# A hybrid attention, convolution and mixture-of-experts layer: the work ahead of the experts in another order, the output gate behind the projection, and softmax and convolution on other engines

## The chip, the cores and the metric

The kernel runs on one core of a Trainium2 chip. The metric is the device time of one execution in microseconds (us). The core's engines are named as in the profile: PE (TensorE: matrix products and transposes), DVE (VectorE), ACT (ScalarE), POOL (GpSimd) and SP (SyncE, which issues nearly all of the transfers). Each engine works through its own list of instructions in the order in which they were written; semaphores hold an instruction back until what it reads is there. The whole list is written by hand here: the code's order is the order on each engine.

## What is computed

One layer on 256 latent tokens (x) and 256 context tokens, 1024 features wide, all float32. It has two parts: a mixer with three groups of heads, and 32 experts.

```python
def trunk_layer(x, xc, mod_x, mod_c, norm1, norm2, w_in, w_fourier, w_conv, rpb, w_out,
                w_rg, b_rg, w_re, b_re, w_gate, w_up, w_down, last):
    ...
    sh1, sc1, g1, sh2, sc2, g2 = jnp.split(mod_x[:, None, :], 6, axis=-1)
    ...
    ux = (rms_norm(x, norm1) * (1 + sc1) + sh1) @ w_in
    uc = (rms_norm(xc, norm1) * (1 + csc1) + csh1) @ w_in
    fx, qx, kx, vx, bx, cx, hx = split_in(ux)
    fc, qc, kc, vc, bc, cc, hc = split_in(uc)
    attn_x = na_latent(qx * scale, kx, vx, kc, vc, rpb)
    conv_x = bx * short_conv(cx * hx, w_conv)
    x = x + g1 * mix_out(fx, attn_x, conv_x, w_fourier, w_out)
    ...
    hx2 = rms_norm(x, norm2) * (1 + sc2) + sh2
    if last:
        y = hier_moe(hx2.reshape(-1, d), w_rg, b_rg, w_re, b_re, w_gate, w_up, w_down)
        x = x + g2 * y.reshape(b, n, d)
```

Here `mod_x = silu(c) @ w_ada + b_ada`, 6144 columns; `w_in` is 1024 x 2560 (256 Fourier, 3 x 512 attention in 8 heads of 64, 3 x 256 convolution); `na_latent` is a softmax over a band of neighbours with a learned bias and all context keys; `short_conv` has width 3; `fourier_mix` is the real part of a two-dimensional Fourier transform, followed by a 256 x 256 product; `w_out` is 1024 x 1024. Each token goes to 2 of the 32 experts (gate and up 1024 x 512, down 512 x 1024 each). The weights of the experts are some 200 MB, all are read once, and the last step is an RMS norm.

## The kernel before

**Weights** come through ten slabs of 2 MB in SBUF (16 KB in each partition). `pump` starts loads in the order of a list, `queue`, as long as a slab is free: `ada0` and `in_0`, `in_1` (first modulation, Fourier columns, outer gate of the convolution, keys), `in_3` (values), `ada1` (four slabs: the gate g1 and the shift of the second norm), `in_2` (queries), `in_4` (the convolution's operands), `small` (constants of the Fourier part and space for intermediate results), `ada2` (four slabs: scale of the second norm and g2), `out_0`, `out_1`, and then for each expert `gu0`, `gu1`, `dn`. `drop` gives a slab back when its last reader is written. A list element that finds no slab holds all that follow, since SP issues in order. An eleventh slab, `more`, is opened shortly before the experts.

**Products with split operands.** Weights of `w_in` and `w_out` are cut into a high and a low part: ACT casts a chunk of 128 x 1024 to a rounded format (L343), DVE subtracts (L344), and the pair lies in one of three buffers `ws`. `ahead(n)` writes casts and splits up to the n-th chunk. `project(i, c, ...)` multiplies a chunk of the input projection by the modulated tokens in three terms (L360), `mix(n)` a chunk of the output projection by the mixer's result `cat` (L517); `mixed` writes two parts of a row block of `cat` (cast on ACT L409, difference on DVE L410).

**Sums.** The modulation that is not needed first is made on DVE: `sums(n)` adds n weighted rows of a slab into an accumulator of 128 x 1024 (L317; L315 for a first row), `acc` for `ada1` and `acc2` for `ada2`; `sum_rows` adds the partitions on PE (L329), `columns` turns a row into columns, and `spread` puts a row on all partitions.

**Attention.** Four pairs of heads. `scores` makes on PE four tiles of 128 x 512 (L467); DVE adds the bias and takes the maximum (two instructions a tile, L473 and L475), ACT the exponential and its sum (L476), DVE the reciprocal (L480) and multiplies by it, the shares (L481). `ptrans` transposes the shares on PE (L488) and ACT copies them to SBUF (L489), `pv` multiplies by the values (L496).

**The order around the change.** Values, queries and the convolution's operands are projected with DVE sums between; then `scores(0, 1)`, the convolution on POOL (L548 to L552), the Fourier products (L539, L544, L569), and the other pairs with the output projection between. POOL multiplies `w_out` by the gate g1 in place (`fold`, L504) before it is cast, so that the projection's result is gated. `x1(t)` adds the residual for half of the tokens (L640), transposes, and makes the second norm (L646, L198, L199); `logits`, `route` and `place` choose the experts; `group` gathers tokens with products (L761), and `hidden` (L792) and `project_down` (L814) are the experts.

## Time and profile before

| what | value |
|---|---|
| median of 3 runs | 645.34 us (644.65 to 646.25) |
| span of the profiled execution | 641.5 us |
| median less span: what lies around the span | 3.84 us |
| PE busy | 476.4 us, 74% |
| DVE busy | 226.8 us, 35% |
| ACT busy | 144.8 us, 23% |
| POOL busy | 44.5 us, 7% |
| moved by DMA | 246.12 MB, mean 384 GB/s |

The span runs from the first to the last instruction of one profiled execution, and shares are of that span. They are averages over two unlike parts: the work ahead of the experts, up to about 204 us, and the experts, which are two thirds of the span. The chain that ended last is, by the page, 62% DMA, 26% PE and 8% DVE.

### The profile page before, as it was taken

How to read it: one execution, taken by the hardware profiler on the slowest of the kernel's cores; microseconds unless marked ns; L12 is line 12 of the kernel's file. 1: busy time of each engine (PE TensorE's matmuls, PEld its weight loads, DVE VectorE, ACT ScalarE, POOL GpSimd, SP SyncE). 2: the span in 40 equal slices, each digit the busy share in tenths (PEclk: the TensorE clock that was granted, in tenths of full speed). 3: DMA queues.
4: the chain of work that ended last, by engine and by line, in shares of the span. 5: the costliest groups of instructions: out<-in, count | busy, mean ns of one | idle time of the engine just before them, and what ended most of it. 6: DMA issues, size and time to landing. Idle time of an engine off the chain costs nothing.

```text
span 641.5 us, 11030 instructions
## 1 busy us (share of the span) xinstructions
PE 476.4 (74%) x4775; PEld 307.9 (48%) x4775; DVE 226.8 (35%) x525; ACT 144.8 (23%) x322; POOL 44.5 (7%) x44
## 2 busy tenths in 40 slices
PE   3999999887987887585567555855946585568785
PEld 3787898544775454253235222632523253235442
DVE  4767877999744222021011000211210021012323
ACT  4524234454642111011001000110100011003003
POOL 1000000894000000000000000000000000000000
PEclk9999999888997999898779778797888888789798
DMA  9999579953797999999999999999999999999992
GB/s 351 422 419 360 222 277 372 428 230 147 295 399 297 429 426 424 426 426 427 426 427 423 425 430 423 422 425 426 424 428 426 425 429 424 426 426 428 423 381 102
DMA packets 21220, 246.12 MB, mean 384 GB/s; under 512 B 2214, under 2 KB 3242, under 8 KB 6956
## 3 DMA queue, kind: packets, MB, share of 16 engines
q1 hardware_dynamic: 21016, 245.08, 91.9%
q8 instruction: 39, 0.64, 0.4%
q10 hardware_dynamic: 148, 0.27, 0.1%
q14 instruction: 17, 0.14, 0.1%
HBM read 244.28 MB, written 1.05 MB: 382 GB/s over the span
## 4 chain that ended last, share of the span: by engine, by line
DMA 62%; PE 26%; DVE 8%; ACT 1%; issue 1%; SPq 1%; DVEq 0%; ACTq 0%
DMA gu<-in_w_gu 41%; DMA dn<-in_w_dn 18%; PE b L360 11%; PE m L792 3%; DMA ada<-in_w_ada 3%; PE b L517 2%; DVE f L317 2%; DVE acc L481 2%; PE m L761 1%; PE m L814 1%; DVE ws L344 1%; PE b L261 1%; PE b L488 1%; PE m L951 1%; DVE acc L475 1%
## 5 line engine op out<-in xcount | busy, mean ns | idle before, releaser
L792 PE MATMUL m<-gu,xg 128*32 128x256 f32 x2048 | 139.9, 425 | 63.8 <-DMA gu<-in_w_gu 60.2
L792 PEld LDWEIGHTS m<-gu,xg 128*32 128x32 f32 x2048 | 72.9, 120 | 125.5 <-DMA gu<-in_w_gu 43.3
L814 PE MATMUL m<-dn,ht 128*32 128x256 f32 x992 | 74.3, 450 | 26.7 <-DMA dn<-in_w_dn 19.6
L802 DVE TENSOR_TENSOR hh<-m,sg 128x128 f32<-128x128 f32 x32 | 9.3, 291 | 182.0 <-ACT sg L800 182.0
L814 PEld LDWEIGHTS m<-dn,ht 128*32 128x32 f32 x992 | 38.8, 125 | 50.5 <-issue 38.5
L822 DVE COPY yg<-m 32x256 f32<-32x256 f32 x56 | 23.4, 418 | 99.1 <-PE m L814 86.8
L822 ACT COPY yg<-m 32x256 f32<-32x256 f32 x56 | 20.4, 364 | 142.8 <-DVE yg L822 142.8
L360 PE MATMUL b<-uh,ws 128*128 128x256 f32 (+1 forms) x224 | 52.1, 317 | 0.1
L800 ACT ACTIVATE sg<-m 128x128 f32<-128x128 f32 x32 | 8.9, 278 | 161.2 <-PE m L792 161.2
L360 PEld LDWEIGHTS b<-uh,ws 128*128 128x128 f32 x224 | 37.0, 188 | 4.7 <-issue 1.2
L360 PE MATMUL b<-ul,ws 128*128 128x256 f32 (+1 forms) x112 | 35.1, 313 | 0.0
L769 POOL TENSOR_TENSOR sw<-st,cmb 128x256 f32<-128x256 f32 x8 | 5.8, 725 | 418.4 <-DVE st L694 293.4
L783 PE MATMUL m<-yg,sl 128*128 128x512 f32 x56 | 27.7, 639 | 6.4 <-ACT yg L822 6.4
L761 PEld LDWEIGHTS m<-sr,xs 128*128 128x128 f32 x224 | 28.7, 208 | 7.7 <-PEq L887 4.8
L761 PE MATMUL m<-sr,xs 128*128 128x128 f32 x224 | 28.9, 292 | 4.0 <-DVE sr L754 4.0
L344 DVE TENSOR_TENSOR ws<-in,ws 128x1024 fp32r<-128x1024 f32 x20 | 24.4, 1221 | 14.9 <-ACT ws L343 14.8
L767 DVE TENSOR_SCALAR xg<-m,a,sh 128x128 f32<-128x128 f32 x32 | 13.1, 410 | 45.4 <-PE m L761 36.9
L804 PE MATMUL m<-ident,hh 128*128 128x128 f32 x32 | 10.9, 340 | 23.7 <-DVE hh L802 23.7
L765 ACT ACTIVATE xg<-m,sh,a 128x128 f32<-128x128 f32 x32 | 14.6, 458 | 59.4 <-DVE xg L767 59.4
L360 PE MATMUL b<-ws,uh 128*128 128x512 f32 (+1 forms) x96 | 25.9, 354 | 1.9 <-ACT uh L300 1.9
L517 PE MATMUL b<-ws,cat 128*128 128x512 f32 x96 | 24.3, 402 | 0.0
L804 PEld LDWEIGHTS m<-ident,hh 128*128 128x128 f32 x32 | 4.6, 143 | 40.9 <-DVE hh L802 40.8
(236 smaller groups left out, 574.4 us busy)
## 6 DMA issues: line engine op xcount, KB each, us to landing
gu<-in_w_gu SPq DMA_DIRECT2D x63, 2048.0 KB, 39.2
dn<-in_w_dn SPq DMA_DIRECT2D x31, 2048.0 KB, 39.1
ada<-in_w_ada SPq DMA_DIRECT2D x12, 2048.0 KB, 9.0
in<-in_w_in SPq DMA_DIRECT2D x3, 2048.0 KB, 11.3
in<-in_w_in SPq DMA_DIRECT2D x8, 512.0 KB, 17.2
out<-in_w_out SPq DMA_DIRECT2D x2, 2048.0 KB, 10.8
gu<-in_w_gu SPq DMA_DIRECT2D x4, 512.0 KB, 32.5
dn<-in_w_dn SPq DMA_DIRECT2D x3, 512.0 KB, 11.5
```

The source lines that it names most:

```text
L317: DVE.scalar_tensor_tensor(a, w, scx[:, j:j + 1], a, op0=OP.mult, op1=OP.add)
L344: DVE.tensor_tensor(ws[:, 1], src, ws[:, 0].bitcast(F32), OP.subtract)
L360: PE.matmul(po, wv if wst else uv, uv if wst else wv, start=(j == 0 and m == 0 and n == 0), stop=(j == NJ - 1 and m == len(parts) - 1 and ...
L517: PE.matmul(yo[t, h], cat[:, a, MIX[n], blk(t)], ws[:, b, h, :], start=(first and k == 0), stop=(last and k == 2))
L761: PE.matmul(pg[:, j, :], xs[:, t, jj * P:(jj + 1) * P], sr[:, t], start=(t == 0), stop=(t == 1))
L765: ACT.activation(xg[:, jj, :], pg[:, j, :], AF.Identity, bias=sh2[:, 0, jj:jj + 1], scale=a2[:, 0, jj:jj + 1])
L767: DVE.tensor_scalar(xg[:, jj, :], pg[:, j, :], a2[:, 0, jj:jj + 1], sh2[:, 0, jj:jj + 1], op0=OP.mult, op1=OP.add)
L783: PE.matmul(yp[2 * t + h], sl[:, t, :], yg[:, blk(h, 512)], start=(g == 0), stop=(g == NE // 4 - 2))
L792: PE.matmul(pg[32 * q:32 * q + 32], xg[:, j, CAP * i:CAP * (i + 1)], wgu[j // 4][:, :, j % 4, q * P:(q + 1) * P], start=(j == 0), stop=(j ...
L804: PE.transpose(pt, hh, ident)
L814: PE.matmul(pd[32 * q:32 * q + 32, :], ht[:, 32 * k:32 * k + 32], wdn[:, q, k, :], start=(k == 0), stop=(k == 3))
L822: (ACT.copy if q % 2 else DVE.tensor_copy)(dst, src)
```

## The change

- **Gate behind the projection.** `fold` is gone; g1 is spread on all partitions late (after pair 3's scores are written) and `x1` multiplies the projection's result by it before the residual is added: one more DVE operation for each half row. The rows of g1 and of the shift are summed in two steps of 256 columns.
- **Shares on ACT.** `shares(m)` holds the reciprocals on DVE and the multiplication as an ACT activation with a scale per partition (L512 of the changed kernel). Half of the PSUM copies of `ptrans` go from ACT to DVE, as does one of the two query copies.
- **Convolution on DVE**, with multiply-and-add in one instruction (`convolve`, L549 to L556).
- **Fourier group beside the values:** `channels`, `positions` and `fourier` stand between the chunks of the value projection, and the `small` operands are loaded earlier for it.
- **Pairs interleaved:** `scores(0)` stands after the first of the four convolution chunks, `scores(1)` before the last, and shares, transposes, sums, casts and products of the pairs follow in turn. All twelve rows of `ada2` that are summed on DVE are summed after the first scores; before, eight of them stood ahead of the attention.
- Not tied to these: the additions of the bias band are half as many and twice as wide, and `sums` stand elsewhere between the values and queries.

```diff
-    queue += [("in", 3, w_in[3])] + first[0:2] + [("in", 2, w_in[2]), first[2], ("in", 4, w_in[4]), first[3]]
-    queue += [("small", 0, small_b)] + [("ada2", t, w_ada[8 + t]) for t in range(2)]
+    queue += [("in", 3, w_in[3]), ("small", 0, small_b)] + first[0:2] + [("in", 2, w_in[2]), first[2], ("in", 4, w_in[4]), first[3]]
+    queue += [("g2", 0, b_g2)] + [("ada2", t, w_ada[8 + t]) for t in range(2)]
...
-    for c in range(4):
-        project(3, c, vals)
-        sums(3)
+    project(3, 0, vals)
+    sums(2)
+    project(3, 1, vals)
+    sums(2)
+    channels()
+    positions()
+    project(3, 2, vals)
+    sums(3)
+    fourier()
+    project(3, 3, vals)
+    sums(3)
...
         project(2, c, quer)
-        sums(1)
+        sums(2 if c < 2 else 1)
...
+    def shares(m):
         for t in range(2):
-            for h in hs:
-                p, mx = pb2[h % 2][:, t, :], ms[h, t]
+            for hh in range(2):
+                p, mx = pb2[hh][:, t, :], stats(2 * m + hh, t)
                 DVE.reciprocal(mx[:, 3:4], mx[:, 2:3])
-                DVE.tensor_scalar(p, p, mx[:, 3:4], None, op0=OP.mult)
...
+                ACT.activation(p, p, AF.Copy, scale=mx[:, 3:4])
...
-                ACT.copy(pt2[h % 2][:, :, blk(t)], pt)
+                (ACT.copy if hh else DVE.tensor_copy)(pt2[hh][:, :, blk(t)], pt)
...
-    def fold(i):
-        for c in range(4):
-            w = loaded["out", i][:, blk(c, D)]
-            POOL.tensor_tensor(w, w, g1b, OP.mult)
...
+    def convolve():
+
+        wc = sa[:, CA["conv"]]
+        ACT.copy(ct, pc)
+        DVE.memset(cp[:, :, 0:SEQ + 2:SEQ + 1], 0.0)
+        DVE.tensor_tensor(cp[:, :, 1:SEQ + 1], ph, ct, OP.mult)
+        for m in range(2):
+            z = ct[:, m, :]
+            DVE.tensor_scalar(z, cp[:, m, 0:SEQ], wc[:, m:m + 1], None, op0=OP.mult)
+            for i in (1, 2):
+                DVE.scalar_tensor_tensor(z, cp[:, m, i:SEQ + i], wc[:, 2 * i + m:2 * i + m + 1], z, op0=OP.mult, op1=OP.add)
+            DVE.tensor_tensor(z, z, gbt[:, m, :], OP.mult)
...
+    project(4, 0, conv)
+    ACT.copy(rg1, sum_rows(acc[:, 0:D], 256, True)[:, 0:256])
+    ACT.copy(r1[:, 0:256], sum_rows(acc[:, D:2 * D], 256)[:, 0:256])
+    ahead(chunks.index(("in", 4, 2)))
+    scores(0)
+    project(4, 1, conv)
...
+    shares(0)
+    sums(2)
+    project(4, 2, conv)
+    sums(2)
+    ptrans(0)
+    scores(1)
+    project(4, 3, conv)
+    drop("uh", "ul")
+    cat = hold("cat", F32R).rearrange("p (s j n) -> p s j n", s=2, j=NJ)
+    pump()
+    convolve()
+    shares(1)
+    ahead(20)
+    pv(0)
+    sums(2)
+    ptrans(1)
+    sums(2)
+    scores(2)
...
+    ahead(21)
+    pv(1)
+    shares(2)
...
     sums(2)
...
+    mix(0)
+    ptrans(2)
     sums(2)
...
+    scores(3)
...
+    mix(1)
...
+    pv(2)
+    shares(3)
...
+    spread(rg1, g1b)
     drop("a")
     pump()
+    mix(2)
+    ptrans(3)
     mix(3)
     mix(4)
-    ahead(27)
-    pv(2)
-    ptrans(6, 7)
     mix(5, (0,))
     pv(3)
...
-            DVE.tensor_tensor(xs[:, t, hs], yo[t, h], xs[:, t, hs], OP.add)
+            DVE.tensor_tensor(junk[:, t, hs], yo[t, h], g1b[:, hs], OP.mult)
+            DVE.tensor_tensor(xs[:, t, hs], junk[:, t, hs], xs[:, t, hs], OP.add)
```

Three places in the order of instructions follow. First ACT around the start of the attention, before: L343 casts a chunk of the convolution's weights (`in_813`), L440 and L275 copy the gate's sums and spread rows, L476 is the exponential, L529 to L545 copy other results.

```order
L343 CAST ws<-in_813 128x1024 x2
L440 COPY g<-b 128x512
L343 CAST ws<-in_813 128x1024
L275 COPY g<-b 128x512 x2
L476 ACT_TABLE_LOAD
L476 ACTIVATE acc,mx<-acc,mx 128x512 x4
L529 COPY f<-b 128x256
L533 COPY g<-b 128x512
```

The same place on ACT in the changed kernel: L341 is the cast, L563 and L564 copy the sums of the gate and the shift, L505 is the exponential, L512 the shares, L520 a copy of transposed shares.

```order
L341 CAST ws<-in_818 128x1024
L563 COPY f<-b 128x256
L564 COPY g<-b 128x256
L341 CAST ws<-in_818 128x1024
L505 ACT_TABLE_LOAD
L505 ACTIVATE acc,mx<-acc,mx 128x512 x4
L512 ACTIVATE acc<-acc,mx 128x512 x4
L341 CAST ws<-in_818 128x1024
L520 COPY f<-b 128x4x128 x2
```

The exponentials moved ahead of the last cast of the convolution's weights, the four shares stand between, and a cast stands behind the two copies of sums.

Second, DVE between the second pair's scores and the third's in the changed kernel: L549 to L556 are the convolution, L511 the reciprocals of the pair that was scored last, L342 the split of the first chunk of `w_out`, L408 a part of `cat`, L315 the sums of `ada2`, L520 copies of transposed shares.

```order
L549 MEMSET g 128x2x2
L550 TENSOR_TENSOR g<-b,g 128x2x256
L553 TENSOR_SCALAR g<-g,sa 128x256
L555 SCALAR_TENSOR_TENSOR g<-g,sa 128x256 x2
L556 TENSOR_TENSOR g<-g 128x256
...
L511 RECIPROCAL mx<-mx 128x1 x4
L342 TENSOR_TENSOR ws<-out_1022,ws 128x1024
L408 TENSOR_TENSOR cat<-b,cat 128x256
L315 SCALAR_TENSOR_TENSOR f<-ada_1_967,scx,f 128x1024 x2
L520 COPY f<-b 128x4x128 x2
```

Before, the reciprocals and the shares stood right behind the first pair's scores on DVE, and of the convolution only its first product (L535) was there:

```order
L480 RECIPROCAL mx<-mx 128x1
L481 TENSOR_SCALAR acc<-acc,mx 128x512
...
L534 MEMSET g 128x2x2
L535 TENSOR_TENSOR g<-b,g 128x2x256
L315 TENSOR_SCALAR f<-ada_2_1079,scx 128x1024
L317 SCALAR_TENSOR_TENSOR f<-ada_2_1079,scx,f 128x1024
```

In the changed kernel the reciprocals stand behind the convolution, and the shares behind them are on another engine.

Third, ACT at the end of the output projection, before: L343 casts chunks of `w_out` (`out_1151` is `out_1`, the number is a buffer's), L409 a part of `cat`, L489 copies transposed shares, L621 loads the table of the square root, L644 is in `x1`.

```order
L476 ACTIVATE acc,mx<-acc,mx 128x512 x4
L343 CAST ws<-out_1151 128x1024 x2
L409 CAST cat<-b 128x256
L489 COPY f<-b 128x4x128 x4
L409 CAST cat<-b 128x256
L621 ACT_TABLE_LOAD
L621 ACTIVATE cst<-cst 128x2
L644 COPY acc<-b 128x4x128
```

And in the changed kernel, from the shares of pair 3: L273 copies the spread gate, `out_1022` is `out_0` and `out_1238` is `out_1`, L640 loads the table.

```order
L512 ACTIVATE acc<-acc,mx 128x512 x4
L273 COPY f<-b 128x256 x4
L341 CAST ws<-out_1022 128x1024
L520 COPY f<-b 128x4x128 x2
L341 CAST ws<-out_1238 128x1024 x3
L407 CAST cat<-b 128x256
L640 ACT_TABLE_LOAD
L640 ACTIVATE cst<-cst 128x2
L341 CAST ws<-out_1238 128x1024
L664 COPY acc<-b 128x4x128
```

Five casts of `w_out` stand behind the last shares now, where two stood behind the last exponentials, and the last of them is behind the table load.

## Rows read from the trace of the kernel before

**Rows 1.** Windows: us; busy PE, PEld, DVE, ACT, POOL; PEclk; DMA share; GB/s.

```profile
116.90:179.90 63.00, 55.61 (x328) 37.82 (x329) 53.21 (x130) 36.45 (x76) 31.05 (x19) 0.92 0.69 273
...
179.90:203.60 23.70, 19.27 (x144) 16.33 (x146) 12.90 (x54) 8.33 (x23) 0.62 (x1) 0.86 0.84 346
203.60:623.00 419.40, 288.89 (x3361) 162.43 (x3353) 69.46 (x180) 47.82 (x131) 6.24 (x11) 0.88 1.00 423
```

**Rows 2.** SP's timeline: start us, us of issuing, transfers (x2 two).

```profile
116.98 8.35 SPq L136 DMA_DIRECT2D gu<-in_w_gu  x2
...
187.38 3.84 SPq L136 DMA_DIRECT2D gu<-in_w_gu  x2
203.64 0.33 SPq L136 DMA_DIRECT2D dn<-in_w_dn  x1
```

**Rows 3.** Chain of waits: start us, us, engine and line.

```profile
113.70 3.26 DVE f L317
...
164.84 5.70 PE b L517 x24
170.54 1.88 PE b L496 x16
```

**Rows 4.** DVE's timeline, first score tile and first residual add.

```profile
116.87 0.41 DVE L473 CUSTOM_DVE_ANT_0 acc<-b,a 128x256 f32<-128x256 f32 x1
...
179.90 1.38 DVE L640 TENSOR_TENSOR xs<-b,xs 128x512 f32<-128x512 f32 x2 [1.44 <-PE b L517]
```

**Rows 5.** PE by lines, 64 to 180 us: busy us, mean ns of one.

```profile
L539 PE MATMUL b<-f 128*128 128x256 f32 x8 | 3.3, 593 | 0.0
L544 PE MATMUL b<-f,g 128*128 128x256 f32 x8 | 2.3, 433 | 0.0
L569 PE MATMUL b<-fr,f 128*128 128x129 f32 (+1 forms) x16 | 2.1, 281 | 0.0
```

**Rows 6.** Windows of 1 us, columns as in the first group.

```profile
116.00:117.00 1.00, 0.00 (x0) 0.00 (x0) 1.00 (x2) 0.00 (x0) 1.00 (x1) 1.00 0.95 410
...
119.00:120.00 1.00, 1.00 (x4) 0.73 (x4) 0.93 (x7) 0.94 (x3) 1.00 (x2) 0.50 0.99 426
```

**Rows 7.** DVE by lines, 64 to 180 us.

```profile
L317 DVE SCALAR_TENSOR_TENSOR acc<-ada,scx,acc 128x1024 f32<-128x1024 f32 x14 | 17.4, 1273 | 0.0
L481 DVE TENSOR_SCALAR acc<-acc,mx 128x512 f32<-128x512 f32 x16 | 16.6, 1035 | 0.6
...
L344 DVE TENSOR_TENSOR ws<-in,ws 128x1024 fp32r<-128x1024 f32 x11 | 13.4, 1218 | 8.9 <-ACT ws L343 8.9
...
L475 DVE CUSTOM_DVE_ANT_0 acc<-b,cst,mx 128x256 f32<-128x256 f32 x16 | 7.7, 484 | 0.6
L473 DVE CUSTOM_DVE_ANT_0 acc<-b,a 128x256 f32<-128x256 f32 x16 | 6.7, 418 | 0.0
...
L410 DVE TENSOR_TENSOR cat<-g,cat 128x256 fp32r<-128x256 f32 x2 | 0.8, 414 | 0.0
...
L640 DVE TENSOR_TENSOR xs<-b,xs 128x512 f32<-128x512 f32 x1 | 0.7, 691 | 1.4 <-PE b L517 1.4
```

**Rows 8.** ACT by lines, 64 to 190 us.

```profile
L476 ACT ACTIVATE acc<-acc,mx 128x512 f32<-128x512 f32 x16 | 11.6, 723 | 13.7 <-DVE mx L475 13.0
L343 ACT CAST ws<-in 128x1024 fp32r<-128x1024 f32 x11 | 11.3, 1051 | 9.6 <-PE b L360 9.6
...
L646 ACT ACTIVATE junk<-xs 128x512 f32<-128x512 f32 x4 | 2.5, 626 | 0.0
...
L621 ACT ACT_TABLE_LOAD x1 | 1.3, 1283 | 0.0
```

**Rows 9.** POOL by lines, 100 to 180 us.

```profile
L504 POOL TENSOR_TENSOR out<-out,g 128x1024 f32<-128x1024 f32 x8 | 21.5, 2710 | 0.0
```

**Rows 10.** L481 on DVE, 140 to 149.3 us and 156 to 180 us: ns minimum/median/maximum.

```profile
L481 DVE TENSOR_SCALAR acc<-acc,mx x4: 851/2390/2428, 140.4 to 146.4; 128x512 f32<-128x512 f32 x4
...
L481 DVE TENSOR_SCALAR acc<-acc,mx x8: 485/486/491, 157.5 to 169.7; 128x512 f32<-128x512 f32 x8
```

200 lines of the change are left out of this document (80 added, 120 removed).

## Prediction, before the changed kernel had run

> **What bounds the kernel now.** I read the windows by stage first [rows 1]: from 203.6 us on the DMA share is 1.00 at 423 GB/s, TensorE (PE) is busy 289 of 419 us, so the experts run at the speed of their weights. Then the load issues of SyncE (SP) [rows 2]: the slab loads of the experts begin at 116.98 and eleven (ten slabs and the eleventh that is opened late) are issued up to the pair at 187.38. The twelfth, at 203.64, must wait until the first expert has read its first slab. In the stage 179.9 to 203.6 the DMA share is only 0.84: the transfers run dry and wait for that read. Everything after is a fixed stream. The span is thus the moment of that read plus 641.5 − 203.6 = 437.9 us, and the change is worth what it does to 203.6. The profiled span of 641.5 goes with the 645.34 median, so 3.84 us lie around it.
>
> What leads to 203.6 is the chain of waits [rows 3]: VectorE (DVE) sums until 113.70 + 3.26, then DVE softmax work, then from 160 PE products (L517), and the router and gather. Its milestones on DVE [rows 4]: the first score tile at 116.87 and the first residual add, x1(0), at 179.90. Between them (63.0 us) DVE is busy 53.2 and waits 9.8; PE is busy 55.6 [rows 1].
>
> **The change, part by part.**
>
> *Start of the attention.* Before, it starts behind the whole projection. After, the first pair's scores stand behind the first convolution chunk. The Fourier products now lie ahead of that on PE, which has no gap there to hide them in: their rows add to 3.3 + 2.3 + 2.1 = 7.7 us [rows 5], but part of that ran at half clock (granted 0.50, its lower level of 1.2 GHz, at 119 to 120, after PE had been idle to 117, [rows 6]); I take 5.3, bounds 4.3 and 7.7. Queries start 4.8 later (91.0 for 86.15), wait about 1.9 for DVE sums, and the first convolution chunk ends at 106.6 instead of 99.9. The gate's row sums take PE to 108.7. ScalarE (ACT) then copies both results before the cast of weight chunk (4,2), whose split DVE must do before the scores: DVE idles 106.7 to 110.1 and starts the first score tile at about **111.2, 5.7 earlier**.
>
> *DVE's work from there to x1(0).* Taken from the 53.2: the 16 shares, 16.6 us [rows 7]. Added: eight sums of the second modulation that were done before 116.9, 8 × 1.24 = 9.9 (L317's 1.27 [rows 7], their ends overlapping); the convolution, about 3.5 (one 0.69 as now, six 128x256 operations on SBUF for which no row exists; bounds 0.25 and 0.5 each by L410's 0.41 [rows 7] and half of it, so 2.9 to 4.7); eight PSUM copies of the transposes, 8 × 0.68 = 5.4 (L640, also 512 from PSUM, 0.69); one more split, 1.2 (L344). Taken: Fourier additions and part of what POOL's contention cost elsewhere, about 2.8 by my adding-up of that stretch (the shares are weighed below). Sum 53.2 − 16.6 + 9.9 + 2.8 + 5.4 + 1.2 − 2.8 = 53.1; walked instruction by instruction 53.8. **DVE's work is the same**; it starts 5.7 earlier.
>
> So x1(0) comes at 111.2 + 53.8 + W = 165.0 + W, W being DVE's waits, 9.8 before. The change is neutral at W = 14.9, less 1.5 for the gate below: 13.4.
>
> *The waits.* I walked the three queues with these durations: score tile 0.87 (0.42 + 0.48, their ends overlapping), exp 0.72 and its read, cast 1.05, share on ACT 0.64. The share has no row; nearest are a 512-wide square of SBUF, 0.63, and exp, 0.72 [rows 8]; with no read behind it I take 0.64, so the bounds are 0.60 and 0.72, or 1.3 us over all 16.
> - Pair 0 to pair 1, 111.2 to 123.6: waits 1.5, mostly for the cast of (4,3), queued on ACT behind the four exps and four shares.
> - Pair 1 to 2, to 143.1: DVE waits 1.5 for ACT's copy of the convolution operand, behind exps; computes the convolution with the reciprocals behind it; so shares(1) start at 132.3 and the cast for the first out chunk, behind them, ends at 135.6: wait 2.8. Meanwhile PE idles 7 us (126 to 133) and 6 us more (137 to 143, the eighth sum). Waits 4.3.
> - Pair 2 to 3, to 158.2: 2.2.
> - From pair 3 on, PE sets the end. After its scores it still has seven products of mix (2.9 each, 24 matmuls took 5.70, [rows 3]; the last three halved), two pv and one set of transposes at 1.9 each (L496; the transposes are taken as alike), and the gate's spread and small sums, 2.5: about 24.7 us; before, all that PE did from this point on stood between 164.84 and 179.90, 15.1 us. It also waits 2 us before pv(2) (the router bias stands on DVE behind a split, whose cast is behind the exps) and 2.9 at the last chunk: its cast is now written behind pv(3)'s copy and the square root's table load (1.28 [rows 8]) on ACT, where before all casts stood ahead of that load. x1(0) at 188.8, DVE waits here 15.8.
>
> W = 1.5 + 4.3 + 2.2 + 15.8 = 23.8. The same walk on the kernel before gives 178.0 for x1(0), measured 179.90: 1.9 short (clock and latencies). I add it: **190.7, 10.8 later**.
>
> *Gate in x1.* Each of four halves gets one more 512-wide DVE operation from PSUM, 0.69 [rows 7]; of the two per token half, bounds 0 (hidden under the transposes) and 1.4; with two token halves one after the other on the chain to the router I take **1.5**, bounds 0.7 and 2.8. Its compensation: POOL's fold (8 x 2.7 us, [rows 9]) goes, off the path itself, but see below.
>
> *Loads.* Slabs three times are freed only by the last mix product (about 196): three loads of 4.9 us end at 211 to 213, just ahead of the first read; they cost nothing now, and would cap the time if compute came earlier. SP's queue is in order: the sixth of the eleven waits behind the fifth, which waits for the first out matrix's last split at 173.9; DMA idles there, but no compute needs those slabs yet. The small operands and the gate's bias move earlier; both were there in time (they are now needed at about 75 and 150).
>
> **Sum.** 203.64 + 10.8 + 1.5 = 215.9; plus 437.9 is a span of 653.8; plus 3.84 is **657.6** by the median: 12 slower, 1.9%.
>
> **A rule against the trace.** [rows 10] show the shares at 487 ns alone and up to 2.4 us while POOL folds (POOL in 112 to 152). The Trainium skill, "SBUF — State Buffer", § Who interferes with whom, says that DVE and GpSimd share one pair of SBUF ports, held exclusively for a whole instruction; the trace agrees (851 to 2428 against 486 ns). By that rule alone removing POOL's work is a gain: see the first rival.
>
> ACT takes over a multiply for which DVE needs 487 ns and a 512-wide ACT row 626 [rows 8, 10]. The Trainium skill, "ScalarE: Activation LUTs", § Rules for kernel authors, would leave a plain multiply on VectorE; by its pricing (about 280 ns + 0.83 ns per column with a pointer operand, § What ACT_TABLE_LOAD costs) a share is an estimated 0.71, 1.1 us more over 16 than I took; no row shows this operation.
>
> **Rivals.**
> 1. *Faster: contention gone.* 16 shares at 0.487 instead of 1.035 would be 8.8 us less; with them on ACT DVE loses all 16.6, and starts 5.7 earlier. If the ACT queue keeps ahead (W about 8), x1(0) is 173 by DVE, but PE needs 24.7 after pair 3, so it must start by 152: 177 at best. With 1.5 for the gate the time is 645.3 − 2.9 + 1.5, about **644**; with PE also packed better, 638. It decides at W < 13.4. For it: 8.8 us of real contention. Against: the four places above, each an order of instructions, not a price. 0.12.
> 2. *Same: the loads hide it*, or W near 13: 645. Against: DMA share 1.00 after 203.6 and none to spare: a late first read is not caught up. 0.06.
> 3. *Slower, but less:* bounds in my favour (Fourier 4.3, convolution 2.9, gate 0.7, no 1.9 added, one of the two PE waits in the tail absent): 215.9 − 6 to 8: **650**. 0.17.
> 4. *Slower still:* PE falls to 1.2 GHz after each idle gap (the fall in [rows 6]), and my walk has two gaps of 6 to 7 us where that one was under 3. Some 5 us of PE work at half clock after each, where PE is on the path: +3 to +6, **663**. 0.13.
> My forecast: 0.52.
>
> **Numbers.** No change means within 0.3%, 1.9 us. Faster 0.12, same 0.06, slower 0.82. The forecast's own range is 652 to 662. For 8 in 10 the lower rivals count: 647 to 664 leaves out rival 1, rival 2 and a bit of rival 4.
>
> **What would show it.** In the changed kernel's profile: first score tile on DVE at 111 (right) or after 114; DVE busy 54 us from there to the first residual; waits of 20 or more named for ACT casts; ACT's last cast right behind the second table load, PE idle before the last product; the twelfth expert load at 214 to 218; DMA share 1.00 from there, 438 us to the end. It is wrong if pair 3's scores begin before 152, if PE's gap around 126 to 143 is absent, or if DMA is full before 203, so that the first read does not set the end.

## The result, and the profile after

The changed kernel takes 663.92 us by the median (661.29 to 665.66, four runs), 1.0294 of the kernel before (95% interval 1.026 to 1.0328; below, the interval stands in brackets behind the ratio): some 19 us slower. Its profiled execution has a span of 660.7 us, with 3.2 us around it.

First the windows of the changed kernel, cut at DVE's first score tile, pair 3's scores, the first residual add and the twelfth expert load (columns as in [rows 1]):

```profile
114.92:197.76 82.84, 64.71 (x383) 44.37 (x381) 52.65 (x136) 42.03 (x82) 0.18 (x1) 0.86 0.66 259
114.92:163.03 48.11, 35.14 (x227) 24.04 (x225) 38.58 (x101) 25.96 (x54) 0.18 (x1) 0.82 0.61 245
163.03:197.76 34.73, 29.57 (x156) 20.33 (x156) 14.07 (x37) 16.06 (x28) 0.00 (x0) 0.91 0.73 279
197.76:222.72 24.96, 17.37 (x139) 14.76 (x143) 15.38 (x58) 8.36 (x23) 0.61 (x1) 0.85 0.78 320
222.72:642.00 419.28, 289.21 (x3361) 161.60 (x3353) 69.50 (x180) 47.79 (x131) 6.40 (x11) 0.87 1.00 423
```

SP's timeline at the twelfth load, which stood at 203.64 [rows 2]:

```profile
207.31 3.68 SPq L137 DMA_DIRECT2D gu<-in_w_gu  x2
222.72 0.33 SPq L137 DMA_DIRECT2D dn<-in_w_dn  x1
```

The load comes 19.08 us later, and from it to the end of the span are 437.98 us, as before: all of the loss lies ahead of it. DMA is full behind it and only 0.78 ahead of it, so that nothing of a late first read is caught up. The window from the residual add to the load grew by 1.2 (23.74 before, 203.64 less 179.90). The rest lies between the scores and the residual add: 82.84 us for 63.0. DVE's work there is what it was (52.65 for 53.21), so its waits went from 9.8 to 30.2.

DVE's timeline, the last split ahead of the scores, the first tile of each pair, the last split of `w_out` and the gate (in brackets the idle time before, and what ended it):

```profile
113.77 1.23 DVE L342 TENSOR_TENSOR ws<-in,ws 128x1024 fp32r<-128x1024 f32 x1 [6.08 <-ACT ws L341]
114.92 0.42 DVE L502 CUSTOM_DVE_ANT_0 acc<-b,a 128x256 f32<-128x256 f32 x1
...
127.62 0.41 DVE L502 CUSTOM_DVE_ANT_0 acc<-b,a 128x256 f32<-128x256 f32 x1
...
148.34 0.42 DVE L502 CUSTOM_DVE_ANT_0 acc<-b,a 128x256 f32<-128x256 f32 x1
...
163.03 0.42 DVE L502 CUSTOM_DVE_ANT_0 acc<-b,a 128x256 f32<-128x256 f32 x1
...
192.44 1.23 DVE L342 TENSOR_TENSOR ws<-out,ws 128x1024 fp32r<-128x1024 f32 x1 [2.02 <-ACT ws L341]
197.76 0.69 DVE L659 TENSOR_TENSOR junk<-b,f 128x512 f32<-128x512 f32 x1 [4.09 <-PE b L543]
```

The waits of DVE and PE in that stretch (total, times, longest):

```profile
DVE ws L342 <- ACT ws L341: 13.9, 7, 3.5
DVE cat L408 <- ACT cat L407: 9.1, 3, 4.3
PE b L519 <- ACT acc L512: 8.2, 1, 8.2
PE b L327 <- DVE f L315: 4.0, 1, 4.0
PE b L615 <- issue: 1.9, 1, 1.9
PE b L622 <- DVE sa L618: 1.8, 1, 1.8
DVE g L550 <- ACT g L548: 1.4, 1, 1.4
```

Some 23 of DVE's 30 us are for casts of ACT, as the prediction had it; none of the waits in that stretch is for a load. But behind pair 3 a DVE wait is mostly the shadow of PE: the parts of `cat` are cast from what PE has just made, and a split waits for a buffer that PE has to read first. What PE did:

```profile
107.51 0.61 PE L326 MATMUL b<-g,ones 1*32 1x256 f32 x2
108.05 0.62 PE L327 MATMUL b<-acc,ones 128*32 128x256 f32 x2
...
111.33 1.05 PE L327 MATMUL b<-acc,ones 128*32 128x256 f32 x10
112.31 1.99 PE L496 MATMUL b<-kv,a 64*128 64x512 f32 x8
...
137.89 3.68 PE L519 MATMUL b<-ident,acc 128*128 128x128 f32 x16 [8.18 <-ACT acc L512]
...
149.40 3.67 PE L600 MATMUL b<-ada,scx 128*32 128x256 f32 x32
...
175.84 3.02 PE L543 MATMUL b<-ws,cat 128*128 128x512 f32 x12
...
193.72 4.00 PE L543 MATMUL b<-ws,cat 128*128 128x512 f32 x11 [0.76 <-DVE ws L342]
```

Three places are to be seen (a count is of matmul records: a plain f32 product has two of them, e7 below has 140 for 70; a product of the split operands has one, as has a transpose). At 107.51 the row sums of gate and shift take 4.9 us, in which a bias row and a sum of the gate alternate, 0.55 apart. At 137.89 PE has stood still for 8.2 us, and runs on at a granted clock of 0.50, its lower level of 1.2 GHz. At 193.72 the last products run at 0.36 us each, where thirty in the middle of this stretch took 7.30, 0.24 each: from 195.0 on the granted clock is 0.50.

The gate in `x1` has a price ahead of its own operations, which the prediction did not count. Its result goes into `junk`, and by the code `junk` is the next of the three `ws` buffers, the one that held the chunk of `mix(5)`; so x1(0) now waits for `mix(5, (1,))` too, six products for the other half of the tokens. Before, x1(0) began at 179.90 [rows 4], 2.0 us ahead of the end of the last eighteen products (first line, 181.93). In e5, the old order with the gate in `x1`, it begins as they end (172.33):

```profile
177.52 4.41 PE L517 MATMUL b<-ws,cat 128*128 128x512 f32 x18
...
167.92 4.41 PE L511 MATMUL b<-ws,cat 128*128 128x512 f32 x18
172.37 0.69 DVE L633 TENSOR_TENSOR junk<-b,f 128x512 f32<-128x512 f32 x1 [3.50 <-PE b L511]
```

In the changed kernel, too, the gate begins (197.76) as the eleven products from 193.72 end (197.72); the six among them took some 2.7 us at a granted clock of 0.50. No run puts `junk` elsewhere.

### The profile page after: what moved, and what is told of

Its sections match the earlier page's. It is cut to its first block, busy times and chain, and to the rows that moved or that the text cites. A ratio compares the mean times of both kernels' runs of the same rounds, so it can differ in the third digit from the quotient of the medians.

```text
span 660.7 us, 11028 instructions
## 1 busy us (share of the span) xinstructions
PE 484.4 (73%) x4789; PEld 311.6 (47%) x4789; DVE 216.9 (33%) x514; ACT 150.6 (23%) x332; POOL 9.3 (1%) x24
## 4 chain that ended last, share of the span: by engine, by line
DMA 58%; PE 26%; DVE 9%; ACT 5%; issue 1%; DVEq 0%; ACTq 0%; SPq 0%
DMA gu<-in_w_gu 40%; DMA dn<-in_w_dn 18%; PE b L358 10%; PE m L812 3%; PE b L543 2%; DVE f L315 2%; ACT acc L505 2%; DVE ws L342 1%; PE m L781 1%; PE b L258 1%; PE m L834 1%; ACT ws L341 1%; PE b L213 1%; PE b L527 1%; PE m L971 1%
## 5 line engine op out<-in xcount | busy, mean ns | idle before, releaser
L812 PE MATMUL m<-gu,xg 128*32 128x256 f32 x2048 | 147.1, 442 | 69.2 <-DMA gu<-in_w_gu 65.6
L812 PEld LDWEIGHTS m<-gu,xg 128*32 128x32 f32 x2048 | 74.9, 124 | 134.9 <-issue 47.6
L834 PE MATMUL m<-dn,ht 128*32 128x256 f32 x992 | 69.6, 427 | 20.8 <-DMA dn<-in_w_dn 13.7
L834 PEld LDWEIGHTS m<-dn,ht 128*32 128x32 f32 x992 | 37.2, 121 | 43.0 <-issue 29.9
L358 PE MATMUL b<-ul,ws 128*128 128x256 f32 (+1 forms) x112 | 35.3, 315 | 0.0
L342 DVE TENSOR_TENSOR ws<-in,ws 128x1024 fp32r<-128x1024 f32 x20 | 24.5, 1224 | 26.9 <-ACT ws L341 26.8
L803 PE MATMUL m<-yg,sl 128*128 128x512 f32 x56 | 25.9, 605 | 6.5 <-ACT yg L842 6.5
L543 PE MATMUL b<-ws,cat 128*128 128x512 f32 x96 | 25.8, 418 | 2.1 <-ACT ws L341 1.3
L358 PEld LDWEIGHTS b<-ul,ws 128*128 128x128 f32 x112 | 21.4, 191 | 1.4 <-DVE ul L300 0.3
```

Source lines behind the costliest of these rows:

```text
L342: DVE.tensor_tensor(ws[:, 1], src, ws[:, 0].bitcast(F32), OP.subtract)
L358: PE.matmul(po, wv if wst else uv, uv if wst else wv, start=(j == 0 and m == 0 and n == 0), stop=(j == NJ - 1 and m == len(parts) - 1 and ...
L543: PE.matmul(yo[t, h], cat[:, a, MIX[n], blk(t)], ws[:, b, h, :], start=(first and k == 0), stop=(last and k == 2))
L803: PE.matmul(yp[2 * t + h], sl[:, t, :], yg[:, blk(h, 512)], start=(g == 0), stop=(g == NE // 4 - 2))
L812: PE.matmul(pg[32 * q:32 * q + 32], xg[:, j, CAP * i:CAP * (i + 1)], wgu[j // 4][:, :, j % 4, q * P:(q + 1) * P], start=(j == 0), stop=(j ...
L834: PE.matmul(pd[32 * q:32 * q + 32, :], ht[:, 32 * k:32 * k + 32], wdn[:, q, k, :], start=(k == 0), stop=(k == 3))
```

## The experiments

Medians are of runs on several chips, so each is told with its ratio to the kernel before on the same chip. In the text, "to x1(0)" is the time from pair 3's first score tile to the first residual operation, 34.7 in the changed kernel and 15.7 before.

**Is POOL's contention real?** e5 is the kernel before with the gate in `x1` and nothing else:

```diff
-            w = loaded["out", i][:, blk(c, D)]
-            POOL.tensor_tensor(w, w, g1b, OP.mult)
...
+    spread(r1, g1b)      # behind mix(1)
...
+            DVE.tensor_tensor(junk[:, t, hs], yo[t, h], g1b[:, hs], OP.mult)
+            DVE.tensor_tensor(xs[:, t, hs], junk[:, t, hs], xs[:, t, hs], OP.add)
```

> The kernel before with one part of the change alone: no folding of the gate into the output weights on POOL, the gate spread on all partitions after mix(1) and multiplied in x1. Convolution (POOL), shares (DVE) and all order stay. Theory: the sums ahead of the first scores (one of them 3.25 us beside the fold, 1.3 alone) and four shares (8.1 us at 140 to 149 beside the fold, 2.0 alone) get back some 8 us of DVE, all on the chain of waits of before; two gate operations more in x1 cost 1.2; the twelfth expert load at 196 to 198.5 for 203.64, time 5 to 7.5 us below the kernel before. Rival, that the contention is covered by PE or by the loads: within 2 us of the kernel before. The cap: three expert loads of 4.9 us have to land, the last slab being freed by x1's last gate operation: not below 196.

Measured: 639.62 us, 0.9919 [0.9891, 0.9947], the fastest of all: 5.2 us ahead of the kernel before. Its windows, and the shares on DVE (L480 here):

```profile
114.03:172.37 58.34, 52.99 (x340) 37.08 (x340) 43.63 (x131) 37.11 (x78) 13.92 (x12) 1.00 0.82 331
154.59:172.37 17.78, 17.74 (x100) 12.60 (x96) 8.82 (x30) 9.54 (x18) 0.00 (x0) 1.00 0.78 290
172.37:197.27 24.90, 17.30 (x139) 14.73 (x143) 15.38 (x58) 8.36 (x23) 0.62 (x1) 0.86 0.73 300
```

```profile
L480 DVE TENSOR_SCALAR acc<-acc,mx 128x512 f32<-128x512 f32 x16 | 8.2, 509 | 0.6
```

The 16 shares cost 8.2 us for 16.6 [rows 7], and of POOL's work only the fold went. The prediction weighed the rule of the Trainium skill, "SBUF — State Buffer", § Who interferes with whom, that DVE and GpSimd hold one pair of ports in turn: the trace agrees (509 ns a share for 1035). Pair 3's scores come 9.6 us earlier than before (154.59 for 164.20); a little of that can be the spread of the gate, which stands later. The gate takes back 3.3 of it by the traces: 2.1 to x1(0), where it waits for `mix(5, (1,))` (17.78 for 15.70), and 1.2 behind it (24.90 for 23.74).

**The moves between engines, or the order?** e10 is e5 with the convolution on DVE, as in the change; e11 is e5 with the shares on ACT; e14 is e5 with both, and with half of the copies of transposed shares on DVE: the moves of the change, save one copy of queries, in the old order. e4 is the changed kernel with the shares back on DVE.

```diff
-                DVE.tensor_scalar(p, p, mx[:, 3:4], None, op0=OP.mult)
+                ACT.activation(p, p, AF.Copy, scale=mx[:, 3:4])          # e11, e14; e4 the reverse
-                ACT.copy(pt2[h % 2][:, :, blk(t)], pt)
+                (ACT.copy if h % 2 else DVE.tensor_copy)(pt2[h % 2][:, :, blk(t)], pt)   # e14
-            POOL.tensor_scalar(y, cp[:, m, i:SEQ + i], wc[:, 2 * i + m:2 * i + m + 1], None, op0=OP.mult)
-            POOL.tensor_tensor(z, z, y, OP.add)
+            DVE.scalar_tensor_tensor(z, cp[:, m, i:SEQ + i], wc[:, 2 * i + m:2 * i + m + 1], z, op0=OP.mult, op1=OP.add)   # e10, e14
```

> The kernel of e5 (before, gate in x1) with the convolution on DVE as in the change, in the place in the order where POOL had it; POOL then does nothing there. Its price by the changed kernel's trace is 3.5 us on DVE (133.3 to 136.9). In e5 DVE has no wait there, and POOL's convolution costs it about 1 us (a share of 0.84, a pair of sums of 3.17 for 2.6). Theory: DVE is the bound there, so x1(0) comes 1.5 to 3 us later than in e5 (172.4), time 641 to 643. Rival, that contention is the main price: faster than e5 (below 639).

> The kernel of e5 with the shares on ACT as in the change, the order left. Shares are 0.61 each on ACT and 0.49 on DVE. Theory of the queues: ACT's copies and casts behind the shares come 2.5 us later for each pair (the convolution operand's copy first), DVE is 2 us freer but waits for them: 0 to 3 us slower than e5. Rival, that DVE's work is the price whatever waits: 2 us or more faster than e5.

> The kernel before with all moves between engines that the change makes (gate in x1, convolution on DVE, shares on ACT, half of the transposes' copies on DVE) but in the order of before: Fourier products behind the first scores, pairs behind the whole projection. The gate alone gave -5.3, convolution on DVE +3.8 and shares on ACT +2.1 upon it. Theory, that the order and not the engines is the loss: 642 to 648 us, the twelfth load at 201 to 206, so 16 to 20 of the 19 us are left for the order. Rival, that moves and order cost alike, since ACT's and DVE's queues get each other's waits: 650 or more.

> The changed kernel with the shares as a multiplication on DVE again (16 of about 0.49, no POOL work beside them), all else left. Theory of the queues: DVE gets 2 us a pair, but the casts of the weights behind the shares on ACT come 2.5 us earlier and take away DVE's waits for them (1.2 and 3.4 us at pairs 0 and 1, 0.7 at pair 2); pair 3's scores within 1.5 us of 163.0 and the twelfth load 221 to 224. Rival, that ACT's price for the shares is the loss: 5 us or more faster. Second rival, that taking the shares off DVE was a gain by itself: 4 us or more slower.

Measured: e10 643.37, 0.9989 [0.9969, 1.0009]; e11 641.67, 0.9955 [0.9941, 0.997]; e14 647.81, 1.0052 [1.0032, 1.0072]; e4 663.34, 1.0277 [1.0243, 1.0312]. So the convolution on DVE gives back 4.5 us of e5's gain, and the shares on ACT 2.3 (the intervals of e5 and e11 just meet); within the new order it makes no difference who multiplies. With these moves the old order is 3.4 us slower than the kernel before. Two expectations were missed: e10 comes to x1(0) 5.3 us later than e5 (177.63), not 1.5 to 3, and e14's twelfth load stands at 208.56, not at 201 to 206. Windows of e14:

```profile
114.87:183.06 68.19, 59.45 (x340) 38.62 (x340) 43.37 (x131) 42.75 (x86) 0.00 (x0) 0.97 0.71 283
163.75:183.06 19.31, 18.59 (x100) 12.88 (x98) 8.15 (x28) 11.01 (x20) 0.00 (x0) 1.00 0.70 265
```

This is the run that divides the loss. It begins its scores when the changed kernel does (114.87 and 114.92) and comes to pair 3 at nearly the same time (163.75 and 163.03). Behind that it needs 19.31 us, PE busy in 18.59 of them, and the changed kernel 34.73. Of 19.0 us, then, 3.4 belong to the moves and 15.6 to the order, with what e14 leaves out: the query copy, the additions of the bias band, and the row sums of the gate in two steps, whose alternating bias rows e3 (below) puts at some 2. Over the whole stretch the order costs 82.84 − 68.19 = 14.65: PE is 5.3 longer busy (43 more matmuls, at a mean granted clock of 0.86 for 0.97) and 9.4 longer idle (18.1 for 8.7).

**The start.** e3 writes all four bias rows of a row sum ahead of the sums. e16 is e5 with the Fourier group beside the values, as in the change. e15 was to be the same, but loads the bias of the second gate over operands that are still read, which changes that gate and holds SP's queue.

```diff
                 PE.matmul(pa[blk(q, 32), 0:n], ones[r, 0:32], bq[r, blk(q % 2, n)], start=True, stop=False)
+        for q in range(4):
             PE.matmul(pa[blk(q, 32), 0:n], ones[:, 0:32], a[:, blk(q, n)], start=not bias, stop=True)
```

```diff
     project(3, 1, vals)
     sums(3)
+    channels()
+    positions()
     project(3, 2, vals)
     sums(3)
+    fourier()
     project(3, 3, vals)
```

> The changed kernel with the gate's row sums written as before: all four bias products first, then the four sums, instead of a bias and a sum for each quarter in turn. In the changed kernel the eight take 4.9 us on PE (107.51 to 112.4), one after the other at 0.55; of the kernel before the eight bias and sum products took about 2.0. Theory of the queues: the first scores start 2 to 2.5 us earlier (112.5 for 114.9), the lead of DVE carries through the pairs and the twelfth load comes 1.5 to 2.5 us earlier. Rival, that a lead at the start is eaten by later waits: load unchanged within 0.7.

> The kernel of e5 with the Fourier group beside the values as in the change, nothing else. PE has no gap there, so the first scores come 4 to 5 us later than in e5 (114.0); behind them DVE has 1.1 us of additions and as much waiting less. Theory: x1(0) 2 to 3 us later than in e5, 641 to 643 us. Rival, that the Fourier products were on the chain behind the scores and come free: below 639.

> e15 mended: there the gate's bias rows were loaded with the small operands, so early that SP held all later loads for the readers of the place they are written to (first scores at 129.1 instead of about 119); here they are loaded apart and later, as the change does. The kernel of e5 with the Fourier group beside the values, nothing else. Theory: PE has no gap there, the first scores come 4 to 5 us later than in e5 (114.0), of which 2 come back behind them; x1(0) 2 to 3 us later than in e5, 641 to 643 us. Rival, that the Fourier products come free: below 639.

Measured: e3 661.44, 1.0251 [1.0216, 1.0285]; e15 653.4, 1.0122 [1.0089, 1.0155]; e16 643.18, 0.9979 [0.9954, 1.0005]. PE's timeline of e3 at the row sums:

```profile
108.70 0.63 PE L326 MATMUL b<-g,ones 1*32 1x256 f32 x8
109.26 1.07 PE L328 MATMUL b<-acc,ones 128*32 128x256 f32 x16
```

The 24 matmuls that took 4.9 us take 1.6, and the first score tile comes at 112.89 for 114.92, although the row sums began 1.2 later. One profile is not enough for that difference: in the eight other runs with the changed kernel's code up to there the tile stands between 113.93 (e4) and 115.90 (e13). But with e3's edit it stands at 111.82 in e8 and at 112.95 in e17 too, so some 2 us are real. x1(0) comes 1.5 earlier, at 196.23, but the load not at all, at 223.33: the six output matmuls at 199.51, ahead of the router, took 2.80 us at a granted clock of 0.50 to 0.54, for 1.63 in the changed kernel. e15's first scores stood at 129.07, a queue held by its own fault; it tells nothing of the question. e16, mended, does. Its windows from the first score tile and from pair 3's on:

```profile
120.60:160.58 39.98, 32.12 (x211) 20.71 (x212) 35.33 (x98) 25.28 (x52) 14.42 (x12) 0.91 0.85 354
160.58:178.36 17.78, 17.74 (x100) 12.60 (x96) 8.82 (x29) 9.54 (x18) 0.00 (x0) 1.00 0.77 288
```

The scores start 6.6 later than in e5, and all but 0.6 of it arrives at x1(0) (178.36 for 172.37); by the medians' ratios it is 3.9. The Fourier products beside the values displace PE work that the scores wait for; where they stood before only 0.6 is won (39.98 us to pair 3 for 40.56 in e5), and the stretch behind it (17.78) is as long. The changed kernel starts its scores no earlier than e14 although it does three chunks of the convolution's projection later: the Fourier group and the alternating row sums have taken that lead.

**The middle.** e1 puts the reciprocals of pair 1 ahead of the convolution. e9 fills PE's gap: the output products of the Fourier rows (`mix(0)`, `mix(1)`) go behind `pv(0)`, those of the convolution's rows into their old places, and four sums behind the convolution.

```diff
-    convolve()
     shares(1)
+    convolve()                                   # e1, in the changed kernel
```

```diff
-    sums(2)                                      # behind shares(0), and behind project(4, 2)
+    ahead(21)
...
+    for o in range(2):
+        mixed(o, yf[:, o, :])
+    pv(0)
+    mix(0)
+    mix(1)
     convolve()
     shares(1)
+    sums(4)
     ptrans(1)
+    sums(4)
     scores(2)
```

> The changed kernel with shares(1) written ahead of the convolution, so that pair 1's reciprocals stand ahead of it on DVE and its shares ahead of the copy of the convolution's operand on ACT. The changed kernel's trace has pair 1's shares at 137.1 us, and PE idle 8.2 us for them (129.7 to 137.9), falling to half clock. Theory of the queues (what stands behind what on DVE and ACT until pair 3's scores, and PE after them): the shares come 5 us earlier and PE's gap moves, but DVE only gains the difference between its wait for the first out cast (3.4 us) and a longer wait for the convolution's operand (now 1.4, then about 4): 1 us or so; the twelfth expert load, 222.7 in the changed kernel, comes at 221 to 222.5. Rival, that PE's idle gap and its half clock are the loss: 5 us of gap go, load at 216 to 218, time 5 us or more below the changed kernel.

> The changed kernel with the output projection's products where PE stands idle: the first two out chunks are cast and split ahead of pair 1's scores (four sums go behind the convolution for it), mix(0) and mix(1) stand behind pv(0) in the gap of 8.2 us, mix(2) and mix(3) take the places of mix(0) and mix(1), so that two products of 2.9 us less are left behind pair 3's scores. Nothing is removed. Theory of the postponed products (the 19 us of the stretch from pair 3's scores to x1(0) are PE products that the kernel before had done by then, while PE now idles 12 us at 130 to 149): the stretch shortens by 5 to 6 us and pair 3's scores (163.0) come no later, x1(0) at 191 to 193, the twelfth load at 216 to 219. Rival, that DVE's waits for ACT or the clock take it back: 221 or later.

Measured: e1 662.81, 1.0272 [1.0235, 1.031]; e9 665.65, 1.032 [1.0289, 1.0352]. In e1 PE's gap moves, and pair 3's scores begin 46.8 us after the first instead of 48.1; nothing of it reaches the load (223.28), and the median is within the interval of the changed kernel's. The rival, 5 us from PE's gap, falls. Windows of e9:

```profile
115.03:168.66 53.63, 42.80 (x251) 28.62 (x249) 41.32 (x103) 27.88 (x56) 0.18 (x1) 0.90 0.62 237
168.66:199.73 31.07, 26.39 (x132) 18.68 (x132) 11.89 (x35) 14.05 (x26) 0.00 (x0) 0.84 0.71 287
```

The stretch behind pair 3 is shorter by 3.7 with 24 matmuls fewer, but pair 3 comes 5.6 later: the window up to it is 5.5 longer, 2.7 of it DVE's work (mostly the two splits that had to come early for those products) and 2.8 DVE's waits.

**The tail.** e2 writes the last cast of `w_out` ahead of the table load. e6 puts the last four sums of `ada2` behind pair 3's scores. e13 is e9 with eight sums there and e2's edit. e17 is the changed kernel with e2's and e3's edits, and four of the sums ahead of the first scores.

```diff
     mix(5, (0,))
+    ahead(27)                                    # e2, e13, e17
     pv(3)
...
+    sums(4)                                      # e17
     ahead(chunks.index(("in", 4, 2)))
     scores(0)
     project(4, 1, conv)
...
     shares(0)
-    sums(2)                                      # e17
     project(4, 2, conv)
-    sums(2)                                      # e17
...
-    sums(2)                                      # e6: ahead of mix(0), and behind ptrans(2)
-    sums(2)
...
     DVE.tensor_copy(lb, pl)
+    sums(4)                                      # e6
```

> The changed kernel with the last out chunk's cast written ahead of pv(3), and so ahead of pv(3)'s copy and of the square root's table load on ACT (1.28 us, 189.98 to 191.26 in the changed kernel). Theory of the queues: the cast then waits only for its buffer and is done by about 187; the two gaps of PE before its last products (1.33 and 0.76 us) go and the products behind them (11 in 4.00 us at half clock) run at full clock in about 2.6: 3 to 3.5 us, the twelfth expert load at 219 to 220. Rival, that the loads or DVE hold the end anyway: no change (within 1 us).

> The changed kernel with the last four sums of the second modulation (the gate g2's, not needed before the last experts) behind pair 3's scores on DVE instead of ahead of them; DVE waits 20 us of the 35 behind that point. Theory of the queues: pair 3's scores start 2.5 to 3 us earlier (then their products on PE stand behind pair 2's transposes), PE's tail starts as much earlier and the twelfth load comes 1.5 to 3 us earlier than in the changed kernel (222.7 to 224.6 in the runs so far). Rival, that PE's clock eats it, as it ate the 2 us of the bias rows: load unchanged within 0.7.

> e9 with eight of the twelve sums (10 us of DVE) behind pair 3's scores, where DVE waited 15 us or more in every run; the row sums, the router's scale and the spread of the gate stand behind them on PE, and the last cast ahead of the table load. e9 shortened the stretch from pair 3's scores to x1(0) from 34.7 to 31.1 us, but its scores came 5.6 us later, DVE being the bound up to them. Theory, that the time is DVE's work up to pair 3's scores plus PE's products behind them, and that either alone only moves the end of the other: pair 3's scores at 159 to 162, the stretch 28 to 32, the twelfth load at 213 to 218, time 654 to 659. Rival, that waits for ACT or SP's order of loads hold the end: 221 or later.

> The changed kernel with three repairs of order: the bias rows apart (e3), the last cast ahead of the table load (e2), and the first four sums of the second modulation ahead of the first scores, where DVE waited 6 us for a cast (107.7 to 113.8), instead of between pairs 0 and 1. No work moves between engines. Theory of the order: first scores at 113.5 to 114.5, pair 3's at 158.5 to 160.5 (163.0 in the changed kernel), the stretch behind it 31 to 33 for 34.7, the twelfth load at 215.5 to 219 for 222.7, time 656 to 660. Rival, that another wait or the clock takes the place of each repair, as for e2 and e3 alone: 221 or later.

Measured: e2 661.69, 1.0251 [1.0212, 1.0291]; e6 669.72, 1.039 [1.0363, 1.0418]; e13 660.48, 1.0234 [1.0203, 1.0265]; e17 656.95, 1.018 [1.0163, 1.0197]. PE's timeline of e2:

```profile
177.06 5.49 PE L543 MATMUL b<-ws,cat 128*128 128x512 f32 x12
...
193.22 4.41 PE L543 MATMUL b<-ws,cat 128*128 128x512 f32 x18
```

The two gaps at the end are gone (18 matmuls in 4.41 at one go), but in this profile the twelve at 177.06 take 5.49 us at a granted clock of 0.50, where they took 3.02 at 1.00, and x1(0) is where it was (197.66). Those twelve stand ahead of the edit, in code that is the same: the edit did not cost this, it is a difference between executions. The profiled one took 663.94 us, the other three 660.22 to 663.14; the median is 2.8 us below the changed kernel's by the ratios, and the intervals overlap. In e6 and e13 there was a new wait, made by where I put the row sums of the late accumulator. They stand on PE ahead of products that were ready, and PE waits for DVE's last sum (e6, then e13):

```profile
176.93 1.08 PE L327 MATMUL b<-f,ones 128*32 128x256 f32 x8 [5.89 <-DVE f L315]
```

```profile
185.99 1.08 PE L327 MATMUL b<-f,ones 128*32 128x256 f32 x8 [3.35 <-DVE f L315]
...
160.36:195.68 35.32, 27.55 (x140) 18.49 (x140) 21.01 (x44) 14.55 (x27) 0.00 (x0) 0.81 0.92 376
```

e6 comes to x1(0) 5.7 later. e13 had pair 3's scores at 160.36, as expected, and then needed 35.3 us where I expected 28 to 32 (its window stands behind its wait); the granted clock there is 0.81, so the wait is only a part of that miss. e17 came out as expected, its first scores (112.95) half a microsecond earlier; its windows:

```profile
112.95:158.56 45.61, 31.72 (x212) 21.32 (x210) 34.17 (x97) 25.73 (x53) 0.18 (x1) 0.89 0.67 265
158.56:190.17 31.61, 30.02 (x156) 21.81 (x156) 14.25 (x37) 16.16 (x28) 0.00 (x0) 0.89 0.70 274
```

Pair 3 comes 4.5 earlier than in the changed kernel, 2.0 of it from the start and 2.5 in the window up to it, where DVE has 4.4 less to do; the load stands at 215.51. Behind pair 3 only 1.6 of 31.61 us are idle; the rest is PE's 156 matmuls, where the old order with the gate in `x1` has 100 (e5, e14).

**The clock.** e7, e8 (e7 with e2's and e3's edits) and e12 keep PE busy in its gaps with products of the identity that nothing reads.

```diff
+    def warm(t, n):
+        for _ in range(n):
+            PE.matmul(t, ident, ident[:, 0:t.shape[-1]], start=True, stop=True)
...
+                if m == 1 and t == 0 and hh == 0:
+                    warm(pt[:, 0, :], 70)        # in ptrans(1), once a slot; e12: 33
+    warm(pl, 14)                                 # ahead of the router's bias; e12: 6; so also in sum_rows, x1, route, group
```

> The changed kernel with products that nothing reads put into PE's gaps, into banks that the next products there overwrite: 70 ahead of pair 1's transposes (gap of 8.2 us), 40 ahead of the row sums for the second norm's scale (4.0), 14 ahead of the router bias (1.9), 4 to 17 between the products of x1 and of the router. They do no work and only keep PE from standing idle. Theory of the clock: the 1.2 GHz stretches behind those gaps go (transposes, scores, gate and pv at half clock, mean granted clock 0.86 between the first scores and x1(0)); DVE bounds the stretch up to pair 3's scores, so those move by less than 1 us, but the tail gets 2 us (pv(2) 2.81 for 1.95, row sums and spread 3.0 for 1.8) and the gather of the tokens 2.3 (5.78 for about 3.5): the twelfth load at 217.5 to 220. Rival, that the clock is off the path: 222 to 224.6 as in the other runs. If the extra products outrun the gaps they push what stands behind them: later than 224.

> e7 together with the two edits that moved their own places but not the end: the last cast ahead of the table load (tail 3 us) and the bias rows apart (start 2 us). Theory of queues and clock together, that each of them had its gain taken by a stretch at 1.2 GHz: with PE kept busy they add up, 4 to 5 + 3 + 2, and the twelfth load comes at 211.5 to 215, 652 to 655 us. Rival, that a further wait takes their place: 216 or later.

> e7 with the idle-gap products counted by their measured price (one takes 0.225 us and not 0.11): 33 ahead of pair 1's transposes, 15, 6, and 1 to 9 in x1 and the router, each set shorter than its gap. Theory of the clock: the stretches at 1.2 GHz behind the gaps go, pair 3's scores stay within 1 us of 163.0, the tail gains about 1.5 to 2, the gather 1.5 to 2: the twelfth load at 218 to 220.5. Rival, that the clock is off the path: 222 to 224.6. If PE falls to 1.2 GHz within a set, the set outruns its gap and the load comes later.

Measured: e7 675.92, 1.0473 [1.0438, 1.0508]; e8 671.9, 1.0424 [1.0395, 1.0453]; e12 665.99, 1.0327 [1.0283, 1.0372]. e7 filled far too much:

```profile
129.28 15.90 PE L366 MATMUL b<-ident 128*128 128x128 f32 x140
```

(70 products, 0.227 us each, 16 us in a gap of 8), and so did e8; of the path they say nothing. But the 16 transposes behind the gap that took 3.68 took 1.91 in e7, and the 32 matmuls of the second gate (L600), 3.67, also 1.91: the price of half clock there. e12 fills about the gaps, and its windows answer the question:

```profile
114.28:162.38 48.10, 43.78 (x323) 32.46 (x321) 38.57 (x100) 25.77 (x54) 0.18 (x1) 0.96 0.61 247
162.38:196.64 34.26, 30.28 (x170) 22.37 (x171) 14.08 (x37) 16.07 (x28) 0.00 (x0) 0.95 0.73 286
196.64:224.47 27.83, 25.41 (x191) 22.90 (x194) 15.38 (x58) 8.37 (x23) 0.62 (x1) 0.82 0.70 281
```

Up to pair 3 the granted clock is 0.96 for 0.82, and the time is the same (48.10 for 48.11): the stretches at half clock behind the two long gaps are off the path. Behind pair 3 it is 0.95 for 0.91, and the stretch is 0.5 shorter. The added products cost more than that in the router, and the load comes at 224.47, not at the 218 to 220.5 that I expected. The clock is a part of the loss, not its main cause.

## Why the prediction came out as it did

The direction, the place and the mechanism were right: DVE's work the same (53.8 said, 52.65 measured), its waits for ACT's casts (23.0), PE's gap in the middle, PE's long work behind pair 3, the last cast behind the table load (192.44, [2.02 <-ACT]), the load as the turning point and 438 us behind it. The size was 12 us, and is 19; the time is past the forecast's own 652 to 662 and at the upper edge of the wider 647 to 664, just outside by the ratio (1.0294 × 645.34 = 664.3). Term by term, 215.9 to 222.72:

| term of the sum | predicted | measured | off by |
|---|---|---|---|
| first score tile | 111.2 | 114.92 | +3.7 |
| first tile to pair 3's | 47.0 | 48.1 | +1.1 |
| pair 3's to x1(0), with the 1.9 added | 32.5 | 34.73 | +2.2 |
| gate in x1 | 1.5 | 1.2 | −0.3 |
| load to the end of the span | 437.9 | 437.98 | 0.1 |

- **The step that failed is the start of the attention**, "The gate's row sums take PE to 108.7". They started at 107.51, 0.9 behind what I took, and lasted 4.9 us, where I took some 2 as in the form before, which has its bias rows first (103.02 to 105.06). Two copies, a cast and a split hang on their end. The granted clock there was 1.00. e3 shows the size: 1.6 us if written apart, and some 2 of lead.
- **The tail was mis-sized by a wait and by the clock.** PE's work behind pair 3, 24.7 in the sum (its terms add to 24.2), was 29.57. The sum has the products of the first half of the tokens; x1(0) also waits for `mix(5, (1,))`, by the code because of `junk`: some 2.7 us. The row sums, the spread and the other small products took 4.6 for 2.5. `pv(2)` took 2.81 for 1.9 and the last eleven matmuls 4.00 for some 2.7 (11 × 0.243), at half clock. I had added 1.9 for clock and latencies, from the kernel before, whose PE has no gap behind pair 3. So the gate's price is not the 1.2 of the table alone.
- **Rival 4** has the time, 663, by luck in the main: the stretches at half clock behind the two long gaps cost nothing (e12), and of the 6.8 us the first two terms carry 4.8 without the clock.
- **Rival 1 (contention gone, faster)** is half true. Without the fold and with the spread later, pair 3's scores come 9.6 us earlier (e5); the gate takes back 3.3, and by the medians 5.2 are left. But it takes one of five parts of the change to have it, and the new order costs 15.6. Its bar, pair 3's scores by 152, was missed by 11.
- **Rival 2** falls (DMA at 0.78 ahead of the load). **Rival 3**'s bounds went the other way, save the gate's own operations: the Fourier products took 5.7 us of PE, the convolution 4.26, and PE's waits in the tail both came.
- **One price was off and moved little, one was right.** The convolution's part on DVE took 4.26 us (132.60 to 136.86), not 3.5: it has eight 128x256 operations, and I had counted six. Its bounds, 2.9 to 4.7, do not follow either: six at 0.25 to 0.5 and the 0.69 give 2.2 to 3.7. DVE's work was still 1.1 under what I said. The share on ACT lasts 711 ns (the mean of 16), but shares in a row overlap: four take 2.55 us, and 16 keep ACT busy for 10.2, the 0.64 each that I took:

```profile
119.24 2.55 ACT L512 ACTIVATE acc<-acc,mx 128x512 f32<-128x512 f32 x4
L512 ACT ACTIVATE acc<-acc,mx 128x512 f32<-128x512 f32 x16 | 10.2, 711 | 6.3 <-DVE mx L511 6.3
```

By the Trainium skill, "ScalarE: Activation LUTs", § What ACT_TABLE_LOAD costs, one share was an estimated 0.71: the trace agrees for one alone. The advice of the Trainium skill, "ScalarE: Activation LUTs", § Rules for kernel authors, to leave a plain multiply on VectorE is borne out in the old order by 2.3 us (e11), at the edge of what was measured, and not in the new one (e4).

What the expected gain of an earlier start came to: the scores stand 1.95 us earlier than before, and e14 has as much in the old order. Interleaving the pairs did not shorten the way to pair 3 (48.1 for 47.3 before). DVE has 5.9 us less to do there (38.58 for 44.45), but waits 9.5 instead of 2.9, mostly for ACT's casts. Before:

```profile
116.87:164.20 47.33, 39.91 (x239) 26.54 (x240) 44.45 (x102) 26.91 (x58) 31.08 (x19) 0.89 0.65 267
```

PE meanwhile ran out of products that it could do, and was left with 156 matmuls for the last stretch instead of 100.

Open remains how the order's 15.6 us divide between the pairs' interleaving and the late sums: e16 gives 3.9 to the Fourier group, e17 gives back 7.4 by three repairs together, and neither part was run alone. The copies on DVE were not run alone either; e14 leaves 1.8 for them and for what the moves do to each other. The 2.8 us that e2 and e3 each show by their ratios lie within the intervals; their traces have no earlier load, but each is of the longest of its four executions.
